# A four-column softmax reciprocal per head pair, and context high and low parts in one matmul in layer 0's MLP

## The chip, the cores and the metric

The kernel runs on one core of a Trainium2 chip, as one program. The metric is the device time of one execution in microseconds (us); lower is better. The core has a matrix engine (TensorE, PE in the profile, whose weight loads are listed apart as PEld), VectorE (DVE), ScalarE (ACT), GpSimd (POOL) and SyncE (SP), which here only issues DMAs. Each engine has its own queue of instructions and waits on semaphores for the others. TensorE writes to PSUM; VectorE and ScalarE read it from there.

## The reference

Two layers over 512 latent tokens and 256 context tokens, width 1024. A layer normalizes and modulates, projects once, runs a gated channel mixer and a grouped-query attention (8 query heads, 2 key and value heads of 64), projects back, and then runs an MLP with a squared relu. Context attends only to context; latents attend to both. The last layer computes latents only, apart from the context's keys and values.

```python
def one_block(qblk):
    s = jnp.einsum('bkgqd,bkmd->bkgqm', qblk, k).astype(jnp.float32)
    p = jax.nn.softmax(s, axis=-1).astype(v.dtype)
    return jnp.einsum('bkgqm,bkmd->bkgqd', p, v)

def sqrelu_mlp(h, w1, w2):
    return jnp.square(jax.nn.relu(h @ w1)) @ w2

for l in range(DEPTH):
    last = l == DEPTH - 1
    ...
    x_lat = x_lat + ga1 * (jnp.concatenate([attn_lat, gm_lat], axis=-1) @ w_out[l])
    x_lat = x_lat + ga2 * sqrelu_mlp(modulate(rmsnorm(x_lat, norm2_g[l]), sh2, sc2), w_ff1[l], w_ff2[l])
    if not last:
        ...
        x_ctx = x_ctx + cga2 * sqrelu_mlp(modulate(rmsnorm(x_ctx, norm2_g[l]), csh2, csc2), w_ff1[l], w_ff2[l])
```

## The kernel before

**Precision by splitting.** Every large product runs in a reduced fp32 format (`F32R`). To keep fp32 accuracy, weights and activations are each split into a high part and a low part (the remainder), and three products are summed in PSUM: high times high, high weight times low activation, low weight times high activation. `fm_mms` (line 631) issues these three for each of the 128-row blocks of the contraction, all into one PSUM region; `mm` (line 216) issues one matmul, so nearly all matmuls stand under line 217. Weights come by DMA on SP's queue as `raw` tiles, ScalarE casts the high part and VectorE or GpSimd subtracts the low part (`split`, lines 221 and 222), into a ring of five. The activations of an MLP layer lie in tiles `[128, 2, T]`: index 0 is the high part, index 1 the low part, and the 768 columns are 512 latents, then 256 context tokens.

**Layer 0's MLP.** The first matrix has 32 output tiles of 128 channels. The first four are made together in `ff1_first`; the other 28 are made by `ff1(m)` (line 1187), each as two column parts of 384 (`DENSE[0]`), 8 blocks times 3 matmuls each, into a two-bank PSUM tile `pa` of which there are two. `relu2` (line 1151) then reads all 768 columns: relu and square on ScalarE, a square and a subtraction on VectorE for the low part. The second matrix runs in 8 chunks of four such tiles. `proj4` (line 978) makes its 8 output tiles for each chunk, in chunks 0 to 6 as a latent part of 512 and a context part of 256, 4 blocks times 3 matmuls each; `gate` (line 971) scales each part and adds it to the residual `X` on VectorE (line 976). Every third output tile uses the small PSUM tiles `pb` and `pt` instead of `pa`. Chunk 7 takes the other path of `proj4`, one bank at a time. The order is: tile 4c+4 of the first matrix, chunk c of the second, tiles 4c+5 to 4c+7, and so on. Between them, `mod_wide` computes the next layer's modulation on ScalarE (line 402) and GpSimd (line 403). In chunks 0 to 6 VectorE and ScalarE take the order in which the code is written; TensorE's and GpSimd's instructions are placed by the framework's scheduler.

**Attention.** `attn_tile` (line 1009) handles one head and 128 queries: scores into `pa`, the negated maximum on VectorE (line 1021), the exponential with its row sum on ScalarE (line 1024), the sum's reciprocal on VectorE (line 1026) and a copy on GpSimd that spreads it over the 64 columns of the head (`rc`, line 1029). Later, after a delay in the planner's virtual time, `second` transposes the exponentials on TensorE (line 1040) into `pt` and splits them (ScalarE line 1042, VectorE line 1043), and `third` multiplies by the values, transposes `rc` (line 1061) and multiplies by it. A pair of heads and two query tiles make four such tiles; layer 0 has 12 of these pairs, layer 1 has 8. Layer 0's output projection and the modulation matmuls (line 354) are fillers between them. In the attention stages the scheduler places the instructions of every engine.

## Time and profile before

| what | value |
|---|---|
| median of 3 runs | 1479.21 us (fastest 1477.65) |
| profiled execution | 1474.87 us, of which its span, first to last instruction, is 1473.1 us |
| granted TensorE clock | 1.000 |
| busy in the span | TensorE 98%, VectorE 59%, ScalarE 43%, GpSimd 25% |
| chain that ended last | TensorE 87%, VectorE 6%, ScalarE 2%, GpSimd 2% |
| DMA | 148.78 MB, mean 101 GB/s |

The busy times come from one profiled execution. A matmul's listed length is longer than its distance to the next one, because matmuls are pipelined and their ends are modelled; what a matmul costs in a row of them is read from the starts. A name such as `pa<-A,hi` says that PSUM tile `pa` is written from tiles `A` and `hi`, with buffer numbers left out.

### The profile page before, as it was taken

To read this page: it belongs to the slowest core of one execution; us is meant where nothing else is said; L and a number is where in the kernel's file an instruction comes from. 1 tells how busy PE (TensorE), PEld (TensorE's weight loads), DVE (VectorE), ACT (ScalarE), POOL (GpSimd) and SP (SyncE) were. 2 spreads that over 40 slices of the span, in tenths; PEclk is the share of its full clock that TensorE was granted. 3 is DMA by queue.
4 is the path that set the end of the run, shared out by engine and by line. 5 is a ranking of instruction groups with operands and counts; after the bars stand their busy time and mean duration, and the time that the engine had idled before them with its cause. 6 is when DMAs were issued, how large, how long until landed. Compare 5 with 4: busy or idle time off the path is not lost.

```text
span 1473.1 us, 21926 instructions
## 1 busy us (share of the span) xinstructions
PE 1443.7 (98%) x8626; PEld 1275.3 (87%) x8626; DVE 875.6 (59%) x1542; ACT 637.2 (43%) x1085; POOL 362.5 (25%) x344
## 2 busy tenths in 40 slices
PE   6999999999999999999999999999999999999998
PEld 3899787888899999998999989998899888888887
DVE  6857867778655454544445437767978554444443
ACT  3552546664545442433324224546865323232221
POOL 0423512222246451313133223265121000000000
PEclk9999999999999999999999999999999999999999
DMA  9322534101233343434243202312002322322331
GB/s 373 111 70 99 196 138 144 58 1 58 94 127 116 119 131 106 130 107 132 92 141 115 99 31 73 101 58 73 15 1 72 117 99 100 100 89 98 101 101 57
DMA packets 50087, 148.78 MB, mean 101 GB/s; under 512 B 5440, under 2 KB 6976, under 8 KB 49984
## 3 DMA queue, kind: packets, MB, share of 16 engines
q1 hardware_dynamic: 49408, 146.72, 29.8%
q8 instruction: 68, 1.11, 0.3%
q10 hardware_dynamic: 576, 0.66, 0.2%
q14 instruction: 35, 0.29, 0.1%
HBM read 145.26 MB, written 2.10 MB: 100 GB/s over the span
## 4 chain that ended last, share of the span: by engine, by line
PE 87%; DVE 6%; ACT 2%; POOL 2%; issue 1%; DMA 1%; SPq 0%; POOLq 0%; ACTq 0%; DVEq 0%
PE pa L217 55%; PE pb L217 23%; PE pt L1040 3%; PE pt L217 2%; PE pb L354 2%; POOL m L298 1%; PE pt L735 1%; DVE lo L222 1%; DMA A<-in_w_mod 1%; POOL lo L222 1%; ACT hi L221 0%; DVE s L897 0%; ACT w L1024 0%; DVE s L706 0%; DVE X L976 0%
## 5 line engine op out<-in xcount | busy, mean ns | idle before, releaser
L217 PE MATMUL pa<-A,hi 128*128 128x384 f32 (+2 forms) x1664 | 440.9, 347 | 1.1 <-DVE s L706 0.9
L221 ACT CAST hi<-raw 128x1024 fp32r<-128x1024 f32 x168 | 176.4, 1051 | 446.4 <-PE pa L217 363.4
L222 DVE TENSOR_TENSOR lo<-raw,hi 128x1024 fp32r<-128x1024 f32 x152 | 191.8, 1262 | 231.1 <-ACT hi L221 227.5
L217 PEld LDWEIGHTS pa<-A,hi 128*128 128x128 f32 x1664 | 299.2, 188 | 22.0 <-DVE s L706 1.1
L217 PE MATMUL pa<-A,lo 128*128 128x384 f32 (+2 forms) x832 | 287.9, 346 | 0.0
L217 PE MATMUL pa<-B,hi 128*128 128x512 f32 (+1 forms) x900 | 240.9, 355 | 0.0
L403 POOL TENSOR_TENSOR C<-C,s 128x512 f32<-128x512 f32 x112 | 163.9, 1479 | 309.8 <-ACT s L402 308.5
L217 PEld LDWEIGHTS pa<-B,hi 128*128 128x128 f32 x900 | 159.7, 189 | 24.1
L217 PEld LDWEIGHTS pa<-A,lo 128*128 128x128 f32 x832 | 156.5, 188 | 10.1
L217 PE MATMUL pa<-B,lo 128*128 128x512 f32 (+1 forms) x450 | 159.5, 355 | 0.0
L217 PE MATMUL pb<-B,hi 128*128 128x512 f32 (+1 forms) x600 | 157.3, 350 | 2.0 <-DVE X L976 2.0
L976 DVE SCALAR_TENSOR_TENSOR X<-pa,modT,X 128x512 f32<-128x512 f32 x126 | 79.4, 658 | 130.5 <-PE pa L217 130.5
L976 DVE SCALAR_TENSOR_TENSOR X<-pb,modT,X 128x512 f32<-128x512 f32 (+3 forms) x116 | 70.8, 619 | 80.8 <-PE pb L217 80.7
L217 PE MATMUL pb<-hi,A 128*128 128x256 f32 (+1 forms) x608 | 118.1, 291 | 0.6 <-DVE m L715 0.6
L217 PEld LDWEIGHTS pb<-B,hi 128*128 128x128 f32 x600 | 103.6, 189 | 16.4 <-DVE X L976 3.0
L217 PE MATMUL pb<-B,lo 128*128 128x512 f32 (+1 forms) x300 | 104.1, 347 | 0.0
L217 PEld LDWEIGHTS pb<-hi,A 128*128 128x128 f32 x608 | 96.9, 191 | 2.2 <-PE pb L217 0.8
L402 ACT ACTIVATE s<-k,silu 128x512 f32<-128x512 f32 x112 | 77.1, 716 | 46.6 <-DMA k<-in_w_mod 33.3
L217 PEld LDWEIGHTS pa<-B,lo 128*128 128x128 f32 x450 | 84.9, 189 | 12.1
L217 PE MATMUL pb<-lo,A 128*128 128x256 f32 (+1 forms) x304 | 87.6, 288 | 0.0
L217 PE MATMUL pb<-A,hi 128*128 128x384 f32 (+2 forms) x288 | 80.4, 361 | 0.9 <-DVE s L823 0.6
L1043 DVE TENSOR_TENSOR A<-pt,A 128x384 fp32r<-128x384 f32 (+1 forms) x144 | 73.1, 536 | 10.2 <-ACT A L1042 8.7
(199 smaller groups left out, 2214.6 us busy)
## 6 DMA issues: line engine op xcount, KB each, us to landing
raw<-in_w_ff SPq DMA_DIRECT2D x128, 512.0 KB, 3.5
k<-in_w_mod SPq DMA_DIRECT2D x96, 256.0 KB, 3.0
raw<-in_w_tok SPq DMA_DIRECT2D x16, 512.0 KB, 3.5
raw<-in_w_out SPq DMA_DIRECT2D x16, 512.0 KB, 3.5
lo<-in_w_mod SPq DMA_DIRECT2D x16, 512.0 KB, 4.7
hi<-in_w_mod SPq DMA_DIRECT2D x16, 512.0 KB, 4.3
A<-in_w_mod SPq DMA_DIRECT2D x8, 512.0 KB, 10.0
B<-in_w_mod SPq DMA_DIRECT2D x8, 512.0 KB, 10.2
```

The source lines that it names most:

```text
L217: pe.matmul(out, a, b, start=start, stop=stop)
L221: act.copy(hi, src)
L222: (eng or vec).tensor_tensor(out=lo, in0=src, in1=hi.bitcast(F32), op=ALU.subtract)
L298: pool_e.tensor_tensor(out=y, in0=v, in1=mhalf[:, 0:n], op=ALU.pow)
L354: pe.matmul(ps[q:q + 32, :], S32[:, k, :], ws_[k2 // 2][:, k2 % 2 * 512:(k2 % 2 + 1) * 512], start=k < ns, stop=k >= KT - ns)
L402: act.activation(p, w, AF.Copy, scale=s)
L403: pool_e.tensor_tensor(out=a, in0=a, in1=p, op=ALU.add)
L735: pe.transpose(p[:, o:o + 128], stk[:, t, hh, c0:c0 + 128].bitcast(F32), ident)
L976: vec.scalar_tensor_tensor(out=xs, in0=src[:, s - off:e - off], scalar=modT[l][:, i * 8 + m, cond:cond + 1], in1=xs, op0=ALU.mult, op1=ALU ...
L1040: pe.transpose(tp_[:, (kt - k0) * 128:(kt - k0) * 128 + 128], p[:, kt * 128:kt * 128 + 128], ident)
L1043: vec.tensor_tensor(out=ptl[:, k0:k0 + step, d], in0=src, in1=pth[:, k0:k0 + step, d].bitcast(F32), op=ALU.subtract)
```

## The change

The change has two parts.

**Softmax.** The four row sums of a head pair go into the four columns of one small tile `sm`. The per-tile reciprocal and copy are taken out. In their place, behind the last tile's transposes in `second`, stands one reciprocal of the four columns and, for each of the two query tiles, one GpSimd copy that spreads both heads' values over 128 columns. `rc` has three buffers instead of four.

**Layer 0's MLP.** The new `pair_mms` computes a context part of 256 columns as two sums side by side in one 512-column PSUM region: one matmul with the high weight reads high and low part of the activation together (512 columns, in two pieces), the other with the low weight adds to the left half. Where the region is read, the two halves are added. `ff1` uses 512 latents with `fm_mms` and 256 context columns with `pair_mms` instead of twice 384, and its reading is written out: ScalarE copies the right half, VectorE adds the left one, and the squares are taken on both engines. `proj4` in chunks 0 to 6 uses `pair_mms` for the context part and adds the halves to the residual one after the other. `ff1_first`, chunk 7 and layer 1's MLP keep their forms.

```diff
--- before.py
+++ after.py
@@ -635,6 +635,16 @@
                 mm(dst, a, b[:, off:off + n], i == 0, i == tot - 1, n)
                 i += 1
 
+    def pair_mms(dst, ws_, Rs, off, n):
+
+        both = dst.rearrange("p (a b) -> p a b", a=2)
+        end = len(Rs) - 1
+        for k, ((whi, wlo, rhi, _), r) in enumerate(zip(ws_, Rs)):
+            one = lambda: mm(both, whi, r[:, :, off:off + n], k == 0, k == end, 2 * n)
+            two = lambda: mm(dst[:, 0:n], wlo, rhi[:, off:off + n], False, False, n)
+            for f in (one, two) if k < end else (two, one):
+                f()
+
     def w8(wb, R):
         whi, wlo = wb
         return [(whi[:, k * 128:k * 128 + 128], wlo[:, k * 128:k * 128 + 128], R[k][:, 0, :], R[k][:, 1, :]) for k in range(KT)]
@@ -991,12 +1001,17 @@
                             if q == 0:
                                 banks = [pb(), pt()] if m % 3 == 2 else (lambda p: [p[:, 0:512], p[:, 512:1024]])(pa())
                             dst = banks[q][:, 0:n]
-                        fm_mms(dst, w4(wbs[m // 2], m, R), off, n)
+                        if bank == "a" and q:
+                            pair_mms(banks[q], w4(wbs[m // 2], m, R), R, off, n)
+                        else:
+                            fm_mms(dst, w4(wbs[m // 2], m, R), off, n)
                         if bank == "b":
                             gate(i, m, off, n, dst)
                         elif q == len(parts) - 1:
-                            for (o_, n_), b_ in zip(parts, banks):
-                                gate(i, m, o_, n_, b_[:, 0:n_])
+                            gate(i, m, *parts[0], banks[0])
+                            if q:
+                                for o_ in (0, n):
+                                    gate(i, m, off, n, banks[1][:, o_:o_ + n])
                         if pi == len(passes) - 1 and q == len(parts) - 1 and m % 2:
                             release()
                         if post:
@@ -1020,13 +1035,10 @@
             nmx = small(1)
             maxes.append(vec.tensor_reduce(out=nmx, in_=ps[:, 0:nk], axis=AX.X, op=ALU.max, negate=True))
             p = tw([128, nk])
-            sm = small(1)
+            if hh == qt == 0:
+                st["sm"] = small(4, tag="sm", bufs=3)
+            sm = st["sm"][:, hh * 2 + qt:hh * 2 + qt + 1]
             act.activation(p, ps[:, 0:nk], AF.Exp, bias=nmx, accum_out=sm)
-            rv = small(1)
-            vec.reciprocal(rv, sm)
-            if hh == 0:
-                st["rc", qt] = small(128, tag="rc", bufs=4)
-            pool_e.tensor_copy(st["rc", qt][:, hh * 64:hh * 64 + 64], rv.broadcast_to([128, 64]))
 
             def second():
                 if qt == 0:
@@ -1042,6 +1054,12 @@
                     act.copy(pth[:, k0:k0 + step, d], src)
                     vec.tensor_tensor(out=ptl[:, k0:k0 + step, d], in0=src, in1=pth[:, k0:k0 + step, d].bitcast(F32), op=ALU.subtract)
                 fl.vt += 110.0 * nkt
+                if hh == qt == 1:
+                    rv = small(4, tag="rv", bufs=2)
+                    vec.reciprocal(rv, st["sm"])
+                    for q in range(2):
+                        st["rc", q] = small(128, tag="rc", bufs=3)
+                        pool_e.tensor_copy(st["rc", q].rearrange("p (h d) -> p h d", h=2), rv.rearrange("p (h q) -> p h q", h=2)[:, :, q:q + 1].broadcast_to([128, 2, 64]))
                 if qt == 1:
                     fl.defer(PAR["PV%d" % l], third)
 
@@ -1188,15 +1206,30 @@
             wb = take("ff1", l, m)
             ps = pa()
             H[m] = unit(hslots[m % 8], [128, 2, T])
-            for i, (off, n) in enumerate(dense):
-                fm_mms(ps[:, i * 512:i * 512 + n], w8(wb, h2), off, n)
+            for i, (off, n) in enumerate(dense if last else ((0, SEQ), (SEQ, CTX))):
+                if i:
+                    pair_mms(ps[:, 512:1024], w8(wb, h2), h2, off, n)
+                else:
+                    fm_mms(ps[:, 0:n], w8(wb, h2), off, n)
                 if i == nd - 1:
                     release()
                 fl.tick()
                 if i == 0:
                     more()
-            src = ps.rearrange("p (a b) -> p a b", a=2)[:, 0:nd, 0:dn] if nd > 1 else ps[:, 0:dn]
-            relu2(m, src, 0, TQ)
+            if last:
+                relu2(m, ps[:, 0:dn], 0, TQ)
+                return
+            hi, lo = H[m][:, 0, 0:T], H[m][:, 1, 0:T]
+            r = tw([128, T])
+            c = r[:, SEQ:T]
+            act.copy(c, ps[:, 768:1024])
+            vec.tensor_tensor(out=c, in0=ps[:, 512:768], in1=c, op=ALU.add)
+            act.activation(r[:, 0:SEQ], ps[:, 0:SEQ], AF.Relu)
+            vec.scalar_tensor_tensor(out=c, in0=c, scalar=0.0, in1=c, op0=ALU.max, op1=ALU.mult)
+            act.activation(hi[:, 0:SEQ], r[:, 0:SEQ], AF.Square)
+            act.copy(hi[:, SEQ:T], c)
+            vec.tensor_tensor(out=r[:, 0:SEQ], in0=r[:, 0:SEQ], in1=r[:, 0:SEQ], op=ALU.mult)
+            vec.tensor_tensor(out=lo, in0=r, in1=hi.bitcast(F32), op=ALU.subtract)
 
         fl.drain()
         with region('ff%d' % l):
```

TensorE, in layer 0's MLP, the end of one first-matrix tile and the start of the next. `pa` is the output, `A` the eight activation blocks (`A_868` to `A_875`), `hi` and `lo` the weights. Before:

```order
L217 MATMUL pa_4968<-A_874_4028,hi_4716 128x384 x2
L217 MATMUL pa_4968<-A_874_4028,lo_4717 128x384
L217 MATMUL pa_4968<-A_875_4029,hi_4716 128x384 x2
L217 MATMUL pa_4968<-A_875_4029,lo_4717 128x384
L217 MATMUL pa_5049<-A_868_4022,hi_4791 128x384 x2
L217 MATMUL pa_5049<-A_868_4022,lo_4792 128x384
```

After the change (the blocks are now `A_796` to `A_803`):

```order
L217 MATMUL pa_4808<-A_801_3895,hi_4577 128x512
L217 MATMUL pa_4808<-A_801_3895,lo_4578 128x256
L217 MATMUL pa_4808<-A_802_3896,hi_4577 128x512
L217 MATMUL pa_4808<-A_802_3896,lo_4578 128x256
L217 MATMUL pa_4808<-A_803_3897,lo_4578 128x256
L217 MATMUL pa_4808<-A_803_3897,hi_4577 128x512
L217 MATMUL pa_4879<-A_796_3890,hi_4646 128x512 x2
L217 MATMUL pa_4879<-A_796_3890,lo_4647 128x512
```

Forty matmuls make a tile where 48 did; the second half alternates between 512 and 256 columns, and the last block has its narrow matmul first.

TensorE again, in the second matrix, the context part of one output tile in `pt`, from four first-matrix tiles (`B`, `C`). Before:

```order
L217 MATMUL pt_5346<-B_971_4593,hi_5033 128x256 x2
L217 MATMUL pt_5346<-B_971_4593,lo_5034 128x256
L217 MATMUL pt_5346<-B_1019_4969,hi_5033 128x256 x2
L217 MATMUL pt_5346<-B_1019_4969,lo_5034 128x256
L217 MATMUL pt_5346<-B_1032_5050,hi_5033 128x256 x2
L217 MATMUL pt_5346<-B_1032_5050,lo_5034 128x256
L217 MATMUL pt_5346<-C_1042_5125,hi_5033 128x256 x2
L217 MATMUL pt_5346<-C_1042_5125,lo_5034 128x256
```

After:

```order
L217 MATMUL pt_5164<-B_899_4461,hi_4907 128x512
L217 MATMUL pt_5164<-B_899_4461,lo_4908 128x256
L217 MATMUL pt_5164<-B_947_4809,hi_4907 128x512
L217 MATMUL pt_5164<-B_947_4809,lo_4908 128x256
L217 MATMUL pt_5164<-B_957_4880,hi_4907 128x512
L217 MATMUL pt_5164<-B_957_4880,lo_4908 128x256
L217 MATMUL pt_5164<-C_967_4951,lo_4908 128x256
L217 MATMUL pt_5164<-C_967_4951,hi_4907 128x512
```

Twelve matmuls of 256 became four of 512 and four of 256; the readers of `pt` stand behind the last.

VectorE in layer 0's attention, where one pair's result `mix` is finished while the next tiles' maxima (`m<-pa`) and subtractions (`A<-pt`) run. Before:

```order
L1026 RECIPROCAL m_3105<-m_3103 128x1
L1021 TENSOR_REDUCE m_3132<-pa_3127 128x1
L1043 TENSOR_TENSOR A_659_3114<-pt_3115,A_658_3113 128x3x128
L1043 TENSOR_TENSOR A_659_3114<-pt_3121,A_658_3113 128x3x128
L1026 RECIPROCAL m_3137<-m_3135 128x1
L1021 TENSOR_REDUCE m_3178<-pa_3173 128x1
L1065 TENSOR_TENSOR mix_3026<-pb_3140,pv_3155 64x256
L1043 TENSOR_TENSOR A_659_3114<-pt_3161,A_658_3113 128x3x128
L1067 TENSOR_TENSOR mix_3026<-pb_3140,mix_3026 128x256
```

After:

```order
L1036 TENSOR_REDUCE m_3014<-pa_3009 128x1
L1036 TENSOR_REDUCE m_3042<-pa_3037 128x1
L1055 TENSOR_TENSOR A_610_3024<-pt_3025,A_609_3023 128x3x128
L1055 TENSOR_TENSOR A_610_3024<-pt_3031,A_609_3023 128x3x128
L1059 RECIPROCAL rv_3159<-sm_2931 128x4
L1083 TENSOR_TENSOR mix_2939<-pb_3046,pv_3061 64x256
L1055 TENSOR_TENSOR A_610_3024<-pt_3067,A_609_3023 128x3x128
L1085 TENSOR_TENSOR mix_2939<-pb_3046,mix_2939 128x256
L1055 TENSOR_TENSOR A_610_3024<-pt_3073,A_609_3023 128x3x128
```

The reciprocals between the maxima (line 1026) are gone from here; one of four columns (`rv<-sm`, line 1059) stands in the stretch, and two maxima follow each other directly.

GpSimd in the same place, where the weights' low parts (`lo<-raw`) share the queue with the `rc` copies. Before:

```order
L222 TENSOR_TENSOR lo_3092<-raw_3089,hi_3091 128x1024
L1029 COPY rc_3018<-m_3016 128x64
L1029 COPY rc_3061<-m_3059 128x64
L222 TENSOR_TENSOR lo_3190<-raw_3187,hi_3189 128x1024
L1029 COPY rc_3018<-m_3105 128x64
L1029 COPY rc_3061<-m_3137 128x64
L222 TENSOR_TENSOR B_118_567<-mix_3026,B_118_567 128x256
L1029 COPY rc_3185<-m_3183 128x64
```

After:

```order
L222 TENSOR_TENSOR lo_3006<-raw_3003,hi_3005 128x1024
L222 TENSOR_TENSOR lo_3092<-raw_3089,hi_3091 128x1024
L1062 COPY rc_3161<-rv_3159 128x128
L1062 COPY rc_3163<-rv_3159 128x128
L222 TENSOR_TENSOR B_118_567<-mix_2939,B_118_567 128x256
L222 TENSOR_TENSOR lo_3183<-raw_3180,hi_3182 128x1024
L222 TENSOR_TENSOR B_118_567<-mix_3130,B_118_567 128x256
```

The copies now come in pairs from one `rv`, behind two low parts here, and fewer of them stand between the low parts.

## The prediction

> **What bounds the kernel now.** I read the page's busy times first, then the stages, then who TensorE waits for, then the chain that ended last and single starts, and last the groups of VectorE, ScalarE and GpSimd that the edits touch. The page's first part gives busy time, share of the span and instructions:
>
> ```profile
> PE 1443.7 (98%) x8626; PEld 1275.3 (87%) x8626; DVE 875.6 (59%) x1542; ACT 637.2 (43%) x1085; POOL 362.5 (25%) x344
> ```
>
> TensorE has 1473.1 - 1443.7 = 29.4 us without work in the whole span. By stage (the columns are the stretch in us, its length, and busy us and instructions of PE, PEld, DVE, ACT and POOL, then granted clock, DMA share and GB/s) these are layer 0's attention, layer 0's MLP, layer 1's attention and layer 1's MLP with its lead-in:
>
> ```profile
> 163.00:361.00 198.00, 194.14 (x1324) 159.38 (x1323) 149.68 (x347) 115.50 (x261) 60.31 (x85) 1.00 0.31 107
> 388.00:860.00 472.00, 471.92 (x2785) 441.39 (x2785) 230.30 (x284) 184.07 (x240) 160.36 (x110) 1.00 0.36 116
> 1000.00:1128.00 128.00, 125.07 (x890) 113.08 (x889) 99.35 (x205) 87.02 (x189) 37.01 (x61) 1.00 0.13 41
> 1128.00:1473.00 345.00, 341.10 (x1560) 284.23 (x1559) 168.56 (x211) 102.45 (x139) 0.00 (x0) 1.00 0.28 94
> ```
>
> In layer 0's MLP TensorE is busy 471.92 of 472.00 us, while VectorE works 230 and ScalarE 184. That stage gets shorter only if its matmuls do. In the attention stages VectorE works 150 of 198 and 99 of 128 us, and TensorE lacks some microseconds. What its weight loads waited for in layer 0's attention (us in total, times, longest) shows how much softmax can give back:
>
> ```profile
> PEld pt L1040 <- DVE A L1043: 4.4, 6, 1.0
> PEld pb L217 <- ACT w L1024: 1.7, 2, 0.8
> PEld pt L1040 <- ACT w L1024: 1.0, 2, 0.8
> ```
>
> The same view over layer 1's attention:
>
> ```profile
> PEld pt L1040 <- DVE A L1043: 2.3, 9, 0.6
> PEld pa L217 <- ACT w L1024: 1.7, 5, 0.6
> ```
>
> Together 4.4 + 1.7 + 1.0 + 2.3 + 1.7 = 11.1 us. The two edits therefore have different ceilings: the MLP edit acts on the bound itself, the softmax edit on at most these waits.
>
> **The MLP edit, on TensorE.** What counts is the distance between starts. The chain of waits (start, length, how many) has whole blocks, the first two in layer 0's second MLP matrix (12 matmuls of 512, then 12 of 256), the third two output tiles of layer 0's first matrix (96 of 384), the last two in layer 1 (24 and 12 of 512):
>
> ```profile
> 416.35 2.75 PE pb L217 x12
> 419.09 1.43 PE pt L217 x12
> ...
> 842.30 16.87 PE pa L217 x96
> ...
> 1156.01 5.44 PE pa L217 x24
> 1161.45 2.72 PE pb L217 x12
> ```
>
> 512 columns cost 5.44/24 = 0.2267 us in an unbroken run and 2.75/12 = 0.2292 right after narrow ones; 256 cost 1.43/12 = 0.1192; 384 cost 16.87/96 = 0.1757 with the changeovers. A straight line through 0.2267 and 0.1192 has 0.42 ns a column and some 12 ns that each matmul costs whatever its width; so the same columns in fewer matmuls cost less. The timeline (start, length, what, how many) gives the inside of a first-matrix tile: 388.38 is the start of its fourth matmul, 396.18 that of the first after its 48th:
>
> ```profile
> 388.38 0.51 PE L217 MATMUL pa<-A,hi 128*128 128x384 f32 x2
> ...
> 396.18 0.63 PE L217 MATMUL pa<-B,hi 128*128 128x512 f32 x2
> ```
>
> It also has a place where wide and narrow alternate, two score tiles of layer 1, 512, 512, 256, 256 and the same again (the row shows only the first shape), up to the transposes behind them:
>
> ```profile
> 1036.66 1.56 PE L217 MATMUL pa<-B,B 128*128 128x512 f32 x8
> 1038.06 0.38 PE L1040 MATMUL pt<-c,w 128*128 128x128 f32 x2
> ```
>
> 384 inside a tile cost (396.18 - 388.38)/45 = 0.1733, and a pair of one 512 and one 256 costs (1038.06 - 1036.66)/4 = 0.350, against 0.2267 + 0.1192 = 0.346 from the blocks.
>
> First matrix, 28 of its 32 tiles (the first four are made elsewhere and stay). Before: 48 of 384, 48 x 0.1733 = 8.32 to 16.87/2 = 8.43 us; I take the middle, 8.37. After: 24 of 512, then eight pairs. The 24 follow narrow ones, so 2.75 + 2.72 = 5.47 (bounds 5.44 and 5.50); the pairs cost 8 x 0.350 = 2.80 (bound below 8 x 0.346 = 2.77). Sum 8.27. Saved 0.10 a tile, 2.8 us in 28; the ends are 8.32 - 8.30 = 0.02 and 8.43 - 8.21 = 0.22, so 0.6 to 6.2 us.
>
> Second matrix, context part, 8 tiles in each of 7 chunks (the eighth chunk takes the other path). Before 1.43 us; after four pairs, 1.40 (1.38). Saved 0.03 to 0.046, times 56: 1.7 to 2.6 us; I take 1.7, since the alternating row is the nearest.
>
> The wide matmul reads its 512 columns in two pieces, high and low half of one tile, which no long matmul of before does. It can't be quicker than 0.2267, the lowest row of one piece. Above I bound it by two matmuls of 256, 0.2384, which is 0.0117 more, for 224 + 224 of them 5.2 us. I take nothing, because the pieces are as long as the 256 columns that alone already stream at their full rate, and keep 5.2 for the range.
>
> A rule speaks against this edit. The Trainium skill, TensorE: Matmul & The Clock Gate, section Back-to-back issue gap, puts the gap of a stream at the columns over 2.4, in ns, plus 2.5. By it a first-matrix tile would go from 48 x 162.5 = 7.80 to 32 x 215.8 + 8 x 109.2 = 7.78 us, by its estimate 0.02 saved, and both matrices together would save 1.1 us, where the rows give 4.5. The trace doesn't agree on the fixed part: 0.2267 us at 512 columns against the rule's 0.2158.
>
> **The MLP edit, beside TensorE.** Nothing new is loaded: the same weights come over SP's queue, and no DMA is issued that was not there. VectorE (by form, busy and mean ns of one):
>
> ```profile
> L1160 DVE TENSOR_TENSOR w<-w 128x768 f32<-128x768 f32 x28 | 26.8, 958 | 13.0 <-ACT B L1159 11.5 <-ACT C L1159 1.4
> L1160 DVE TENSOR_TENSOR w<-w 128x512 f32<-128x512 f32 x32 | 22.0, 692 | 3.7 <-ACT C L1159 3.3 <-ACT B L1159 0.4
> L1161 DVE TENSOR_TENSOR B<-w,B 128x768 fp32r<-128x768 f32 x24 | 36.6, 1525 | 0.8
> L1161 DVE TENSOR_TENSOR B<-w,B 128x256 fp32r<-128x256 f32 x12 | 4.8, 419 | 0.1
> L1065 DVE TENSOR_TENSOR mix<-pb,pv 64x256 f32<-64x256 f32 x40 | 16.6, 414 | 10.6 <-ACT pv L1064 9.4 <-POOL B L222 0.4 <-POOL acc L479 0.4
> L976 DVE SCALAR_TENSOR_TENSOR X<-pa,modT,X 128x256 f32<-128x256 f32 x42 | 20.0, 475 | 0.0
> ```
>
> Before, a tile takes 0.96 + 1.53 = 2.48 us. After: the sum of the halves, 256 out of PSUM, 0.41; relu-square of the context, 256, 0.42; the square of the latents, 512, 0.69; the subtraction unchanged, 1.53; together 3.05. That is 0.57 more, 16 us in 28 tiles. In the second matrix the context is added in two steps, 56 more of 0.475 us, 27 us. VectorE goes from 230 to about 273 of some 468 us. ScalarE:
>
> ```profile
> L1154 ACT ACTIVATE w<-pa 128x768 f32<-128x768 f32 x28 | 22.5, 804 | 4.6 <-PE pa L217 4.6
> L1154 ACT ACTIVATE w<-pa 128x512 f32<-128x512 f32 x30 | 17.6, 591 | 3.5 <-PE pa L217 3.5
> L1154 ACT ACTIVATE w<-pa 128x256 f32<-128x256 f32 x10 | 3.6, 381 | 2.5 <-PE pa L217 1.4 <-DVE B L1161 1.1
> L1159 ACT ACTIVATE B<-w 128x768 fp32r<-128x768 f32 x24 | 20.4, 849 | 0.8
> L1159 ACT ACTIVATE B<-w 128x512 fp32r<-128x512 f32 x28 | 17.5, 634 | 0.8
> L1159 ACT ACTIVATE B<-w 128x256 fp32r<-128x256 f32 x12 | 4.8, 417 | 0.1
> ```
>
> 0.80 + 0.85 = 1.65 becomes 0.38 + 0.59 + 0.63 + 0.42 = 2.02, so 10 us in 28 tiles, 184 to 194. I cost all this at nothing. The cover is TensorE's own next tile: PSUM tile `pa` has two buffers, so its reader has 8.3 us before the buffer is wanted; before, that was one ScalarE read of 0.80, now copy, relu and VectorE's sum, about 1.0 with the last two side by side. VectorE's sum is now queued behind ScalarE's copy, and what stands behind it on VectorE (the low parts of the next weights, the residual adds) waits about 0.4 us longer; both feed TensorE one tile or more later. If that cover were gone, the price would be the 1.0 us on each of 28 tiles.
>
> **The softmax edit.** Per tile a reciprocal and a copy go; per pair of heads (20 of them) one reciprocal of four columns and two copies of twice the width come, placed behind the last tile's transposes:
>
> ```profile
> L1026 DVE RECIPROCAL m<-m 128x1 f32<-128x1 f32 x80 | 12.8, 160 | 18.6 <-ACT w L1024 17.6
> ```
>
> On GpSimd the copies, and the weights' low parts that share its queue:
>
> ```profile
> L1029 POOL COPY rc<-m 128x64 f32<-128x64 f32 x80 | 20.8, 261 | 130.7 <-DVE m L1026 125.9 <-PE pb L1061 3.0 <-PE pb L217 1.7
> L222 POOL TENSOR_TENSOR lo<-raw,hi 128x1024 fp32r<-128x1024 f32 x16 | 38.6, 2417 | 18.1 <-ACT hi L221 18.1
> ```
>
> Who waited in the whole span around them:
>
> ```profile
> POOL rc L1029 <- DVE m L1026: 125.9, 55, 4.6
> DVE m L1026 <- ACT w L1024: 17.6, 33, 1.7
> ```
>
> VectorE loses 80 x 0.16 = 12.8 us and 17.6 us of standing still in front of the reciprocal until the exponentials are summed; it gains 20 x 0.16 = 3.2. GpSimd's 20.8 us become 40 copies of between 0.26 (price by instruction) and 0.52 (by width), 10 to 21 us; either way GpSimd isn't the bound. VectorE's next score maximum and the subtraction that frees the transposes' bank come earlier, and these are what TensorE waits for in the rows above. The gain is at most those 11.1 us. At the other end, the reciprocal's copies may be late for the two transposes of the inverse sums: they stand behind a weight's low part on GpSimd (2.42 us) at three places of layer 0 in the new order of GpSimd's queue, and with the copies themselves (0.16 + 2 x 0.52 = 1.2) that is 3.6 us each, 11 us if nothing covers it. But the pair's 12 matmuls and, in the order, another tile's scores stand in front of those transposes, so most is covered. The scheduler also places the layer 0 fillers anew between scores and transposes, which can go either way. I take 1 us gained, near zero because TensorE is busy 194 of the 198 us there, and keep -11 to +11.
>
> **Sum.** 2.8 + 1.7 + 1.0 = 5.5 us, against the profiled execution's own 1474.87 us (span 1473.1 and 1.8 around it): 1469.4. The median of the runs shown is 1479.21, 0.3% above the profiled one, and the fastest timed run is 1477.65. The mean of 1474.87, 1477.65 and 1479.21 is 1477.2; less 5.5 it is 1472, which I forecast.
>
> **Rivals.** (1) The two pieces cost 0.0117 each, 5.2 us, and eat the 4.5 of the MLP. For it: the saving of a first-matrix tile is a difference of 0.1 between numbers of 8.3. Against it: 384, 512 and 256 columns lie on one line, and a tile needs 8 matmuls less. With softmax's 1 us the time is 1477.
> (2) The fixed part doesn't go with the count: a wide matmul after a narrow one costs what its columns cost, as three narrow ones, 3 x 0.1192 = 0.358 a pair instead of 0.350. That is 0.008 x 448 = 3.6 us of the 4.5, time 1475. Against it: the alternating row itself. The Trainium skill's page TensorE: Matmul & The Clock Gate, section Back-to-back issue gap, would end near here, with 1.1 us saved.
> (3) Softmax gives all it can: the 11.1 us of waits go beside the MLP's 4.5, 1477.2 - 15.6 = 1462. Against it: most of them name the transposes' bank, whose readers on ScalarE and VectorE stay.
> (4) Softmax costs: late copies stop TensorE for 11 us, 1477.2 - 4.5 + 11 = 1484. For it: GpSimd's queue. Against it: the work ahead of those transposes.
> (5) Slower: the read in two pieces breaks the stream. From 78 ns on top of 0.2267 it decides: 448 x 0.078 = 35 us eat the 5.5 and add 29.6, which is 2%. At twice the time it is 448 x 0.2267 = 102 us, 1574. For it: no long matmul of before reads in two pieces, so no row excludes it. Against it: runs of 256 columns have their full rate.
>
> **How the numbers follow.** I give the forecast 0.60, rival (1) 0.12, (2) 0.07, (3) 0.07, (4) 0.08, (5) 0.06. The forecast's own ends are 0.6 + 1.7 and 6.2 + 2.6 us on the MLP, 1468 to 1475, and 0.3% between executions lies on top, 4 us. The range 1462 to 1485 takes these in with rivals (1) to (4); (5) lies outside. Over 2% is 29.6 us, about what a measurement of this kernel can tell from no change. Faster by that is more than the 8.8 and 11.1 us of both edits' upper ends: 0.02. Slower by that is rival (5), 0.06. Within 2% is the rest, 0.92.
>
> **What would show it.** In the changed profile: 8,626 - 448 = 8,178 matmuls; in layer 0's MLP a first-matrix tile of 40 matmuls in about 8.27 us and a context part of 8 in about 1.40; the stage some 4.5 us shorter with TensorE still at its full share, VectorE near 273 us; wide two-piece matmuls 0.227 to 0.24 apart. In the attention stages fewer waits on the transposes' bank and none of TensorE on `rc`. The prediction is wrong if the wide ones are more than 0.24 apart, if TensorE waits for `pa` or for `rc`, or if the attention stages move by more than the MLP.

## The result and the profile after

Both kernels were run six times on one chip. One of the six runs of before took 3305.47 us; it is among the three behind the 1479.21 of the table of before, and the ratio leaves it out. Medians: 1478.05 us before, 1473.2 us after (1472.49 to 1474.03); the ratio of after to before is 0.9968 with a 95% interval of 0.9954 to 0.9981. The time is 4.9 us shorter, inside the range and 1.2 us above the 1472 that was forecast. The profiled execution took 1474.03 us, its span 1471.9.

The page's first part, after:

```profile
PE 1440.3 (98%) x8178; PEld 1225.0 (83%) x8178; DVE 909.6 (62%) x1594; ACT 642.3 (44%) x1141; POOL 364.6 (25%) x304
```

TensorE has the 448 matmuls less that were counted, and is 1471.9 - 1440.3 = 31.6 us without work, against 29.4 before. The stages, with the columns of the table by stage shown of before (layer 0's attention, layer 0's MLP, layer 1's attention, layer 1's MLP with its lead-in):

```profile
163.00:361.00 198.00, 192.89 (x1325) 159.22 (x1324) 146.06 (x315) 115.64 (x263) 55.49 (x61) 0.99 0.30 107
388.00:857.00 469.00, 468.88 (x2341) 391.59 (x2340) 270.91 (x395) 190.86 (x296) 171.47 (x110) 1.00 0.34 117
997.00:1125.00 128.00, 123.64 (x881) 111.87 (x880) 97.96 (x179) 86.79 (x189) 33.64 (x44) 1.00 0.11 38
1125.00:1472.00 347.00, 342.41 (x1570) 285.41 (x1568) 168.94 (x212) 102.47 (x139) 0.71 (x1) 1.00 0.27 94
```

In layer 0's MLP TensorE is full as before, with VectorE at 271 us and ScalarE at 191. Fixed stretches cut stages at different instructions, so the gain is better read between instructions that both kernels have. I use four stretches, in us: A, from layer 0's first score tile to its last; B, from there to the last of the small modulation matmuls of line 421, which lie inside layer 0's MLP; C, from there to the long run of projection matmuls that follows layer 1's attention; D, from there to the last matmul. The column "half clock" says how many us inside A the TensorE clock was at half (the last section is on that). These numbers are worked out from the starts of the matmuls in the traces, those of the experiments included:

```
kernel                            A       half clock   B        C        D
before                            157.97   0           521.43   250.21   376.46
e4 before_again                   160.33   6.8         521.45   250.21   376.47
after                             158.24   3.4         517.60   251.54   376.53
e1 mlp_only                       157.78   0           517.63   250.46   376.48
e2 soft_only                      157.76   3.4         521.44   252.18   376.48
e3 grouped                        157.10   0           516.10   252.30   376.51
e5 grouped_old_softmax            158.79   3.4         516.09   250.60   376.46
e6 softmax_layer_0                158.39   3.4         516.07   250.86   376.51
e7 softmax_layer_1                160.45   6.8         516.09   251.93   376.46
e8 more_reads                     157.33   0           518.34   251.42   376.48
e9 last_pair_old                  157.32   0           516.11   252.77   376.47
```

From before to after, B loses 3.83 us, C gains 1.33, and D is the same to 0.07. A can only be compared at an equal number of half-clocked us. The MLP edit gave 3.83 of the 4.5 us that were forecast; the softmax edit is a matter of A and C, and that takes the experiments.

Inside the MLP the gain is small for each tile. The timeline of a first-matrix tile after (start, length, what, how many), from its first context matmul, at 443.69, to the last one at 446.26; the second matmul of the last row is the next tile's first, and starts at 446.50:

```profile
443.69 0.39 PE L217 MATMUL pa<-A,hi 128*128 128x512 f32 x1
443.91 0.28 PE L217 MATMUL pa<-A,lo 128*128 128x256 f32 x1
444.02 0.40 PE L217 MATMUL pa<-A,hi 128*128 128x512 f32 x1
444.26 0.28 PE L217 MATMUL pa<-A,lo 128*128 128x256 f32 x1
...
446.26 0.63 PE L217 MATMUL pa<-A,hi 128*128 128x512 f32 x2
```

Eight pairs take 446.50 - 443.69 = 2.81 us, 0.351 each. A wide matmul behind a narrow one takes 444.26 - 444.02 = 0.24. The medians over the tiles whose records are complete, again worked out from starts (after the change and in e3 a first-matrix tile is given as its 512 latents plus its context pairs):

```
us                                        before            after             grouped (e3)
first matrix, one tile                    8.320             5.461 + 2.813     5.468 + 2.766
second matrix, latents + context          2.748 + 1.432     2.727 + 1.407     2.747 + 1.379
```

### The profile page after: what moved, and what is told of

It is laid out like the page before. It is cut to its first block, busy times and chain, and to the rows that moved or that the text cites. A ratio compares the mean times of both kernels' runs of the same rounds, so it can differ in the third digit from the quotient of the medians.

```text
span 1471.9 us, 21047 instructions
## 1 busy us (share of the span) xinstructions
PE 1440.3 (98%) x8178; PEld 1225.0 (83%) x8178; DVE 909.6 (62%) x1594; ACT 642.3 (44%) x1141; POOL 364.6 (25%) x304
## 4 chain that ended last, share of the span: by engine, by line
PE 86%; DVE 6%; ACT 3%; POOL 2%; issue 1%; DMA 1%; SPq 0%; POOLq 0%; ACTq 0%; DVEq 0%
PE pa L217 54%; PE pb L217 23%; PE pt L1052 3%; PE pb L354 2%; PE pt L217 2%; POOL m L298 1%; PE pt L745 1%; ACT w L1041 1%; DMA A<-in_w_mod 1%; POOL lo L222 1%; DVE lo L222 1%; ACT hi L221 0%; DVE s L907 0%; ACT A L1054 0%; DVE A L795 0%
## 5 line engine op out<-in xcount | busy, mean ns | idle before, releaser
L217 PE MATMUL pa<-A,hi 128*128 128x512 f32 (+2 forms) x1440 | 430.0, 376 | 0.7 <-DVE s L716 0.4
L217 PEld LDWEIGHTS pa<-A,hi 128*128 128x128 f32 x1440 | 262.8, 188 | 46.8 <-DVE s L716 0.7
L217 PE MATMUL pa<-A,lo 128*128 128x512 f32 (+2 forms) x832 | 283.8, 347 | 0.0
L222 DVE TENSOR_TENSOR lo<-raw,hi 128x1024 fp32r<-128x1024 f32 x152 | 202.5, 1332 | 122.2 <-ACT hi L221 117.8
L403 POOL TENSOR_TENSOR C<-C,s 128x512 f32<-128x512 f32 x112 | 175.0, 1577 | 295.1 <-ACT s L402 288.3
L217 PE MATMUL pa<-B,hi 128*128 128x512 f32 x750 | 239.0, 391 | 0.0
L986 DVE SCALAR_TENSOR_TENSOR X<-pa,modT,X 128x512 f32<-128x512 f32 x168 | 99.8, 615 | 105.6 <-PE pa L217 104.1
L217 PEld LDWEIGHTS pa<-B,hi 128*128 128x128 f32 x750 | 139.9, 188 | 27.1
L217 PE MATMUL pa<-B,lo 128*128 128x512 f32 (+1 forms) x450 | 155.2, 354 | 0.0
```

What stands on the lines that cost most here:

```text
L217: pe.matmul(out, a, b, start=start, stop=stop)
L222: (eng or vec).tensor_tensor(out=lo, in0=src, in1=hi.bitcast(F32), op=ALU.subtract)
L403: pool_e.tensor_tensor(out=a, in0=a, in1=p, op=ALU.add)
L986: vec.scalar_tensor_tensor(out=xs, in0=src[:, s - off:e - off], scalar=modT[l][:, i * 8 + m, cond:cond + 1], in1=xs, op0=ALU.mult, op1=ALU ...
```

## The experiments

Ratios are to the kernel before, run beside each on the same chip. The diffs are against the changed kernel where nothing else is said; three dots stand for lines left out.

**e4, the kernel before again, as a control.** No edit.

> The kernel before, unchanged, for a second profile and the scatter between executions. All theories: ratio 1.000 within 0.001. If the 3 us between the profiled 1474.87 and the median 1478.05 of the kernel before are chance of one execution, this profile lies near 1478, and the trace shows where the 3 us are (granted clock below full speed for a few us in the first 180 us, or a later start); if a profile is always faster, it is again near 1475.

Measured: 1477.42 us, ratio 1.0001 (0.9992 to 1.0010). So with this many runs (eleven, and 28 of before beside them) a difference below some 1.5 us can't be told from nothing, while the stretches tell much smaller ones; the 29.6 us that the prediction gave as the limit was far too much. The table says why one execution tells less than its stretches: its B, C and D are within 0.02 us of those of before, and A differs by 2.4 us.

**e1, the MLP part alone.** The softmax is as before.

```diff
-            if hh == qt == 0:
-                st["sm"] = small(4, tag="sm", bufs=3)
-            sm = st["sm"][:, hh * 2 + qt:hh * 2 + qt + 1]
+            sm = small(1)
             act.activation(p, ps[:, 0:nk], AF.Exp, bias=nmx, accum_out=sm)
+            rv = small(1)
+            vec.reciprocal(rv, sm)
+            if hh == 0:
+                st["rc", qt] = small(128, tag="rc", bufs=4)
+            pool_e.tensor_copy(st["rc", qt][:, hh * 64:hh * 64 + 64], rv.broadcast_to([128, 64]))
...
-                if hh == qt == 1:
-                    rv = small(4, tag="rv", bufs=2)
-                    vec.reciprocal(rv, st["sm"])
...
```

> The change's MLP part alone, softmax as before. My theory (the MLP carries the gain, softmax about nothing): 448 matmuls fewer, layer 0's MLP between its first and last small modulation matmuls 3 to 5 us shorter, time 1473 to 1475, ratio about 0.997 to before. Rival (softmax carries half): 1476, ratio 0.9985. In its profile the pair of one wide and one narrow matmul costs about 0.352 us, as in the change's profile (235 and 117 ns by its starts).

Measured: 1473.37 us, ratio 0.9978 (0.9969 to 0.9987). The median is 4.0 us below the 1477.34 beside it; by the ratio it is 3.2 us (1.9 to 4.6). B is 517.63 as in the changed kernel, 3.8 less than before; C is 250.46, as before. The MLP part carries the gain.

**e2, the softmax part alone.** `ff1`, its reading and `proj4` are as before.

```diff
-                        if bank == "a" and q:
-                            pair_mms(banks[q], w4(wbs[m // 2], m, R), R, off, n)
-                        else:
-                            fm_mms(dst, w4(wbs[m // 2], m, R), off, n)
+                        fm_mms(dst, w4(wbs[m // 2], m, R), off, n)
...
```

> The change's softmax part alone, MLP as before. My theory: 1476.5 to 1478.5, ratio 0.999 to 1.000; layer 1's attention about 1.6 us longer than before as in the change's profile, layer 0's the same or 1 us shorter. Rival (softmax carries half of the gain): 1475 to 1476, ratio 0.9985 or lower. Rival (softmax costs and hides a part of the MLP's gain): 1479 or more, ratio above 1.0005.

Measured: 1476.54 us, ratio 1.0000 (0.9991 to 1.0009): no change that can be told. The table shows that this nothing is made of two parts: C is 252.18 against 250.21 before, 2 us lost around layer 1's attention, and A is 157.76 with 3.4 us at half clock, where before takes 157.97 with none.

**e3, the wide matmuls of a context part side by side.** The same matmuls as in the changed kernel; of each context part first all wide ones, then all narrow ones, instead of in turns.

```diff
-        for k, ((whi, wlo, rhi, _), r) in enumerate(zip(ws_, Rs)):
-            one = lambda: mm(both, whi, r[:, :, off:off + n], k == 0, k == end, 2 * n)
-            two = lambda: mm(dst[:, 0:n], wlo, rhi[:, off:off + n], False, False, n)
-            for f in (one, two) if k < end else (two, one):
-                f()
+        for k, ((whi, _, _, _), r) in enumerate(zip(ws_, Rs)):
+            mm(both, whi, r[:, :, off:off + n], k == 0, False, 2 * n)
+        for k, (_, wlo, rhi, _) in enumerate(ws_):
+            mm(dst[:, 0:n], wlo, rhi[:, off:off + n], False, k == end, n)
```

> The change, with a context part's wide matmuls first and its narrow ones behind them, so that the width changes once and not at each matmul; the same matmuls. If changing the width is what makes a pair cost 0.352 instead of 0.346 us: a first-matrix tile 8.23 us instead of 8.30, a context part of the second matrix 1.38 instead of 1.405, together 3 us less, 1470. If the read in two pieces is what costs: the wide ones stay at 0.235 us and the time at 1473.

Measured: 1471.8 us, ratio 0.9970 (0.9959 to 0.9982), with B 1.5 us shorter than in the changed kernel. The timeline of e3, from a tile's context part to the next tile:

```profile
433.99 1.98 PE L217 MATMUL pa<-A,hi 128*128 128x512 f32 x8
435.81 1.11 PE L217 MATMUL pa<-A,lo 128*128 128x256 f32 x8
436.76 0.63 PE L217 MATMUL pa<-A,hi 128*128 128x512 f32 x2
```

The eight wide matmuls, each reading two pieces, are (435.81 - 433.99)/8 = 0.2275 us apart, what 512 columns in one piece cost in an unbroken run before (0.2267). The two pieces cost nothing that shows. The eight narrow ones are 0.119 apart, so a wide and a narrow one cost 0.346, not the 0.352 (the median, 2.813/8) of taking turns. Taking turns is what costs, some 6 ns a pair. Tile and context part came out as expected (5.468 + 2.766 = 8.23 and 1.38 us), but the gain is half of the 3 us expected: the tile in turns was 8.274, not 8.30, and the latents behind a context part are back at 2.747 us, since they start behind a narrow matmul again.

**e5, e3's MLP with before's softmax in both layers.** The edits of e1 and e3 together.

> The MLP part with its wide matmuls side by side, as in e3, but with before's softmax in both layers. Stage theory: what the parts do adds up. Layer 0's MLP, from the first to the last of the modulation matmuls in it, takes 408.5 us as in e3 (409.9 in the changed kernel, 413.3 before); the stretch from layer 1's last score tile to the first long projection block takes 8.47 us as before (9.90 in e3); layer 0's attention is about 0.9 us longer than in e3. Time about 1472, ratio about 0.9965. Rival (the softmax part is a net gain and the two parts help each other): the time is 1 us or more above e3's 1471.8, 1473 or more.

Measured: 1470.75 us, ratio 0.9958 (0.9945 to 0.9970). B is 516.09 as in e3 and C is back at 250.60, and the stretch from layer 1's last score tile to the projection block is 8.46 us, as expected. The parts add up, and the rival, by which they help each other, falls: nothing is lost with the new softmax gone.

**e6 and e7, the new softmax in one layer.** As e5, with the new form in layer 0 alone (e6) or in layer 1 alone (e7); `sm` has two buffers, `rv` one and `rc` four. The diff is that of e6 against e5; in e7 the condition is `l == 1`.

```diff
-            sm = small(1)
-            act.activation(p, ps[:, 0:nk], AF.Exp, bias=nmx, accum_out=sm)
...
+            if l == 0:
+                if hh == qt == 0:
+                    st["sm"] = small(4, tag="sm", bufs=2)
+                sm = st["sm"][:, hh * 2 + qt:hh * 2 + qt + 1]
+                act.activation(p, ps[:, 0:nk], AF.Exp, bias=nmx, accum_out=sm)
+            else:
+                sm = small(1)
...
+                if l == 0 and hh == qt == 1:
+                    rv = small(4, tag="rv", bufs=1)
```

> As e5, with the new softmax form in layer 0 alone (two buffers of sums, one of reciprocals, four of rc). Stage theory: the form gains about 0.9 us in layer 0's attention, where projection and modulation matmuls fill between the tiles, and loses 1 to 2 us in layer 1, where the last head pair's reciprocal and copies lie behind its last transposes. So this is the fastest of all: 0.5 to 1 us below e5, about 1471, layer 1's stretch at 8.47 us. Rival (layer 0's 0.9 us is only scatter of the clock near 180 us): the same as e5 within 0.3 us.

> As e5, with the new softmax form in layer 1 alone. Stage theory: layer 1's stretch between the last score tile and the long projection block goes from 8.47 to 9.90 us and the time is 1 to 2 us above e5, 1473 to 1474. Rival (the order of the whole of layer 1's attention is what changed, not the form): the stretch stays near 8.5 us and the time is that of e5.

Measured: e6 1469.7 us, ratio 0.9953 (0.9940 to 0.9965); e7 1472.2 us, ratio 0.9967 (0.9957 to 0.9978). The order e6, e5, e7 is the one expected, but the intervals overlap, and the table decides. C is 250.86 in e6 and 251.93 in e7, and the stretch from the last score tile to the projection block is 8.47 and 9.90 us, as expected. The buffers aren't what does it, since e6 and e7 have the same numbers of them. Over all kernels, C is 250.21 to 250.86 (mean 250.47) in the five with the old form in layer 1, and 251.42 to 252.30 (mean 251.87) in the five with the new one: 1.4 us lost, without an overlap. A is 157.97 and 157.78 with the old form in layer 0 and no half-clocked us, 157.10, 157.33 and 157.32 with the new one; with 3.4 us at half clock 158.79 against 158.24, 157.76 and 158.39. That is 0.6 and 0.7 us gained; the second rests on one trace of the old form, and the three of the new one differ by 0.6 among themselves. (At 6.8 us only the old form was seen, 160.33 and 160.45.) e6 is the fastest of all kernels here by its median, before and after among them.

What TensorE waits for in layer 1's attention (us in total, times, longest) is, in e6:

```profile
PE pa L217 <- ACT w L1044: 0.2, 1, 0.2
```

and in e7:

```profile
PE pa L217 <- ACT w L1041: 2.0, 4, 0.8
```

Score tiles have to wait until an exponential has freed their `pa` bank. All kernels with the old form there wait 0.2 us for it, and those with the new form in layer 1 wait 1.8 or 2.0. ScalarE shows the other half, its waits in the same stretch, first in e6 and then in e7:

```profile
ACT A L1062 <- PE pt L1060: 6.0, 13, 0.9
```

```profile
ACT A L1062 <- PE pt L1060: 8.7, 17, 1.0
```

In e7 ScalarE stands longer in front of casts of transposes that TensorE hasn't made, with an exponential queued behind. The timeline of e7 has one such place; the brackets give the wait ahead of the instruction:

```profile
1061.67 0.48 ACT L1062 CAST A<-pt 128x384 fp32r<-128x384 f32 x1 [0.57 <-PE pt L1060]
1062.04 0.41 ACT L221 CAST B<-mix 128x256 fp32r<-128x256 f32 x1
1062.35 0.48 ACT L1062 CAST A<-pt 128x384 fp32r<-128x384 f32 x1
1062.86 0.37 ACT L1090 COPY pv<-pb 64x256 f32<-64x256 f32 x1
1063.25 0.90 ACT L1041 ACTIVATE w<-pa,m 128x768 f32<-128x768 f32 x1
```

TensorE's next score tile starts when that exponential has read its bank:

```profile
1064.30 0.51 PE L217 MATMUL pa<-B,B 128*128 128x512 f32 x1 [0.83 <-ACT w L1041]
```

How much of the 1.4 us is this wait can only be argued. Over all of C TensorE is without work for 3.4 to 3.7 us in the five kernels with the old form, and for 5.4 to 6.5 us in the six with the new one, e9 of the next paragraph among them (the length of C less TensorE's busy time in it); 1.6 to 1.8 us of the difference are the wait for `pa`. But the time isn't longer where the wait stands: from layer 1's first score tile to its last it is 90.1 to 91.0 us with the new form and 90.8 to 91.4 with the old. It is longer behind the last score tile, 9.9 us (10.4 in e9) against 8.46 to 8.48, where the new order has left 24 transposes instead of 18 to be done. Waits and order of work changed together, and no run changes one of them alone.

**e9, only layer 1's last head pair in the old form.** The new form everywhere else, on e7's basis.

```diff
-            if l == 1:
+            if not l or j < 3 or blk == 0:
...
-                if l == 1 and hh == qt == 1:
+                if (not l or j < 3 or blk == 0) and hh == qt == 1:
```

> As e7 with the new softmax form in both layers, apart from the last head pair of layer 1, which keeps before's form. Theory (layer 1's loss stands at its end alone, where the last pair's transposes, reciprocal and copies have no other tile beside them): the stretch from the last score tile to the long projection block is back at 8.47 us, the sum from the last modulation matmul of layer 0's MLP to that block back at 250.2 to 250.9 us, and the time that of e6, 1470 within 1. Rival (the form costs in all of layer 1's attention, where there are no filler matmuls, or the order of its tiles does): the sum stays near 251.9, the time 1471 or more.

Measured: 1472.46 us, ratio 0.9971 (0.9959 to 0.9983). C is 252.77, no shorter than with the new form throughout, and the stretch from the last score tile to the projection block is 10.40 us instead of the 8.47 expected. My theory, that the last pair's reciprocal and copies make the loss because nothing stands beside them, falls: with the last pair in the old form the end is longer still, and as many transposes (24) are left behind the last score tile. The wait is still there, in e9's waits of layer 1's attention:

```profile
PE pa L217 <- ACT w L1041: 1.8, 3, 0.8
```

**e8, two and a half times the reading.** The changed kernel, with the right half of each context part added four times.

```diff
-                                for o_ in (0, n):
+                                for o_ in (0, n, n, n, n):
                                     gate(i, m, off, n, banks[1][:, o_:o_ + n])
```

> The changed kernel, but the right half of each context part of the second matrix in layer 0's chunks 0 to 6 is added to the residual four times instead of once: 56 times 3 more reads of the same bank on VectorE, so that context's MLP output is another than the reference's. By the 0.3 us of one such addition this is some 50 us more of VectorE work inside a stage in which it is busy for 271 of 469 us. Theory of the prediction (the additional reading is hidden as long as TensorE has another bank to write): the time stays at the changed kernel's 1473, within 1 us, with VectorE near 320 us in that stage. Rival (each later release of a bank pushes TensorE): with 1 us per output tile, up to 56 us more; anything over 1480 speaks for it.

Measured: 1472.53 us, ratio 0.9968 (0.9956 to 0.9980), the changed kernel's time. The stage of layer 0's MLP in e8:

```profile
388.00:857.00 469.00, 468.62 (x2338) 390.81 (x2337) 347.85 (x564) 189.94 (x294) 167.73 (x110) 1.00 0.36 117
```

VectorE has 347.85 - 270.91 = 76.9 us more work there, more than the 50 I had worked out, because an addition takes 0.46 us rather than 0.3 (the prediction's own row had 0.475), and TensorE is as full as ever. B is 0.7 us longer. To within that, the cover holds for almost three times the work that the change added.

## Why the prediction was right, point by point

**The bound.** That layer 0's MLP gets shorter only if its matmuls do, and that their readers don't count, is shown by B in e1 and, to within 0.7 us, by e8. Not only their number counts: e3 has the same matmuls in another order and is 1.5 us shorter there.

**First matrix, 2.8 us.** It gave 28 x (8.320 - 8.274) = 1.3. The tile of after is right, 8.274 us for 8.27. The tile of before is what was mis-sized: I took 8.37, the middle between the rows inside a tile (8.32) and a chain row of two tiles with changeovers (8.43); nine of the sixteen tiles with complete records have 8.320. The other seven have 8.41 to 8.46, but such additions are there after the change too (5.55 to 5.61 instead of 5.461 for the latents), so they drop out of the difference. I had put them on one side only, and a difference of 0.1 can't bear an error of 0.05 on one side.

**Second matrix, 1.7 us.** The context part went from 1.432 to 1.407, 0.025 saved, 1.4 us in 56, near the 0.03. What was not in the sum is the latent part behind it, 2.748 to 2.727: a context part now ends in a wide matmul, and so the next latents no longer start behind a narrow one. That is another 1.2 us. Together 28 x 0.046 + 56 x 0.046 = 3.9 us, against 4.5 forecast and 3.83 seen in B.

**The two pieces, taken at nothing.** Right, by e3; rivals (1) and (5) are out. Rival (2), no saving a pair, is out as well, though taking turns costs more than the 0.350 by which I sized it: the eight pairs take a median 2.813 us, 0.352 each, where 0.358 would have been no saving. The rule that the prediction sets beside it, from the Trainium skill, TensorE: Matmul & The Clock Gate, Back-to-back issue gap, is given in that section for an isolated matmul, not for a stream; for a stream the section has about 131 ns at 512 columns. The trace agrees with neither, with 226.7 ns in an unbroken run and 3.83 us saved in B where the rule gave 1.1.

**VectorE and ScalarE at nothing.** They were expected at about 273 and 194 us in the stage and are at 271 and 191. By form, in the stage after, the residual's additions from `pa`, the relu-square, the sum of the halves and ScalarE's copy (busy us, mean ns, idle before):

```profile
L986 DVE SCALAR_TENSOR_TENSOR X<-pa,modT,X 128x256 f32<-128x256 f32 x84 | 40.3, 479 | 1.5
L1228 DVE SCALAR_TENSOR_TENSOR w<-w 128x256 f32<-128x256 f32 x27 | 14.2, 528 | 0.9
L1226 DVE TENSOR_TENSOR w<-pa,w 128x256 f32<-128x256 f32 x28 | 11.9, 425 | 89.0 <-ACT w L1225 89.0
L1225 ACT COPY w<-pa 128x256 f32<-128x256 f32 x28 | 10.4, 372 | 118.8 <-PE pa L217 118.8
```

The sum is queued behind ScalarE's copy and stands 89 us in front of it, but both wait for TensorE's tile, so that costs nothing. The relu-square took 0.53 us, not 0.42.

**Softmax, 1 us gained.** The sign was wrong: 0.6 to 0.7 us gained in layer 0, 1.4 lost in layer 1, so about 0.7 lost by the stretches; the times of e1, e2 and the changed kernel can't tell that from nothing. Rival (3) is out. The arithmetic of the engines was right. After, the whole span has

```profile
L1062 POOL COPY rc<-rv 128x128 f32<-128x128 f32 x40 | 11.3, 310 | 78.7 <-DVE rv L1059 57.5 <-DVE A L441 10.1 <-PE pt L1052 8.0
L1059 DVE RECIPROCAL rv<-sm 128x4 f32<-128x4 f32 x20 | 3.4, 171 | 2.7 <-ACT w L1041 2.5
```

The reciprocal of four columns costs 0.17 us, that of one 0.16; GpSimd's copies went from 20.8 to 11.3 us, VectorE stands 2.5 us in front of the reciprocal instead of 17.6, and no wait of TensorE on `rc` shows. So rival (4) by its mechanism, late copies, is out. The step that failed is that I looked at those copies for the loss, and gave the new order of the queues only a clause, for the fillers of layer 0. What came with the loss is that new order in layer 1: transposes left behind the last score tile, and a new wait, that of score tiles for a `pa` bank. "TensorE waits for `pa`" stood among the signs of a wrong prediction, and it came, in layer 1's attention. A second sign, wide matmuls more than 0.24 us apart, was just reached: in the first matrix they are 0.226 to 0.241 apart. The waits that softmax was to give back didn't go either. The five rows of before added up to 11.1 us; the same five now add up to 4.4 + 1.7 + 0.8 + 1.7 + 3.9 = 12.5. The first of layer 0's stands as it was, and the second of layer 1's, 1.7 before, has grown:

```profile
PEld pt L1052 <- DVE A L1055: 4.4, 7, 1.0
```

```profile
PEld pa L217 <- ACT w L1041: 3.9, 7, 1.0
```

From which waits layer 0's 0.6 to 0.7 us came I have not found; the half-clocked windows lie in the same stretch and shift its waits from one execution to the next.

That the wait for `pa` goes with the new form in layer 1 is shown by all eleven traces. That it is what makes C longer isn't shown, and why the scheduler queues the casts ahead of the exponentials there isn't either: moving the last pair back didn't undo it, and an order written by hand wasn't tried.

**The number.** 3.8 gained in the MLP and 0.7 lost in softmax make 3.1 us by the stretches. The medians differ by 4.9, with an interval of 2.8 to 6.8 us, which holds both the 3.1 and the forecast of 5.5; what lies between is inside the scatter. By the stretches the forecast had 0.7 us too much in the MLP and 1.7 too much in softmax. The base of 1477.2 was also 0.9 us below the 1478.05 that was measured. That 1472 came within 1.2 us of 1473.2 is thus partly luck.

## What to carry to other kernels

Where an engine is full, and the others have slack, fewer and wider instructions pay by the fixed part of each, and their order pays too: keep instructions of one width side by side. Size a small difference from rows of one kind, inside a tile on both sides, and count the instruction behind the changed block as well. Where a scheduler places the instructions, taking work out of one form moves the order of all queues, and that can cost more than the work was worth, in one place and not in another; try such a form place by place.

## What the hardware showed that I had not expected

**Width changes.** Behind a narrow matmul a wide one takes 0.236 us (the median) instead of 0.227, and the narrow one behind it 0.117 instead of 0.119, so a pair taken in turns costs some 6 ns more than the 0.346 of e3.

**The clock.** The scatter between executions goes in large part with the TensorE clock: of the 28 runs of before beside e1 to e4, those with a mean granted clock of 1.000 took 1474.8 to 1476.9 us, those with 0.996 took 1478.0 to 1479.4. In windows of 3.4 or 6.8 us it ran at half speed, at two places: near 20 us, and between 177 and 192 us, in layer 0's attention. Busy times and granted clock by stretch, with the columns as above, first of after, then of the kernel before as e4, each time the 3.4 us ahead of the half-clocked window and a stretch with the window in it:

```profile
174.70:178.10 3.40, 1.61 (x16) 0.43 (x17) 3.40 (x7) 0.56 (x2) 3.40 (x5) 1.00 0.99 382
177.00:182.00 5.00, 4.28 (x25) 1.18 (x26) 3.08 (x11) 1.83 (x5) 1.92 (x2) 0.66 0.42 157
```

```profile
181.10:184.50 3.40, 1.92 (x15) 1.55 (x13) 3.34 (x8) 1.36 (x3) 0.91 (x2) 1.00 0.82 253
184.00:192.00 8.00, 8.00 (x43) 7.54 (x43) 6.53 (x17) 5.39 (x17) 1.21 (x3) 0.57 0.40 143
```

A granted clock of 0.66 over 5 us is 3.4 us at half speed: 1 - 0.5 x 3.4/5. In the profiled execution of before there was no such window. One window in stretch A goes with some 0.9 us (157.88 to 158.79 in the old form), two with 2.5. The Trainium skill, TensorE: Matmul & The Clock Gate, Part 1, says that the clock of a single busy core is either full or half, and decided over windows of 3.4 us; the trace agrees with both. It says that an idle window brings the half clock. Here it took less than that: in the 3.4 us ahead of each of the six half-clocked windows near 180 us (after, e2, e4, e5, e6, e7) TensorE was busy for 1.6 to 2.1 us, about half the time. But in e3 it was busy for only 1.77 us there and kept the full clock:

```profile
174.10:177.50 3.40, 1.77 (x18) 0.76 (x19) 3.40 (x6) 0.74 (x2) 3.40 (x4) 1.00 0.93 367
```

So a half-empty window goes with the half clock, and what decides in a given execution stays open.
